# Down projection of the ConvFFN by seven block products, with block sums made by accumulating transfers

## The chip, the cores and the metric

The kernel runs on one core of a Trainium2 chip. The metric is the device time of one execution in microseconds. Before the change the median of three runs is 1632.61 us (1627.53 to 1633.84).

## The reference, cut to what matters

One layer over 1024 latent tokens of width 1024: modulated input, two attention branches (a windowed and a global one), gates, output projection, LayerNorm, then a gated ConvFFN with D_FF = 2816 and a second LayerNorm. The change lies in the ConvFFN.

```python
def _conv_ffn(h, w_up, conv_w, conv_b, w_down):
    u = h @ w_up                                   # (1024, 5632)
    u = conv_of_width_3_over_tokens(u) + conv_b
    gate, val = jnp.split(u, 2, axis=-1)
    return (jax.nn.silu(gate) * val) @ w_down      # (1024, 2816) @ (2816, 1024)

h = x * (1.0 + scale2) + shift2
y = _conv_ffn(h, w_up[l], conv_w[l], conv_b[l], w_down[l])
x = _layer_norm(DEEPNORM_ALPHA * x + gate2 * y, ln2_g[l], ln2_b[l])
```

## The kernel before, in words

Everything is kept transposed, with features on the 128 partitions and tokens along the row. A product of fp32 matrices is made of three matmuls (`mm3`, L85 to L88): each operand is split into a rounded high part, cast on ACT (L78), and the low rest, a subtraction on DVE or POOL (L83), and high by high, high by low and low by high are summed in one PSUM bank.

The program goes through projections, 32 attention units (`Unit`, L378; 16 of the windowed branch, then 16 of the global one, in a loop over u that interleaves the steps of scores, values and filling work), branch merge, LN1, and the ConvFFN. In an attention unit SP writes a row of sums to DRAM (`dn`, L497), reads it back spread over partitions (`rb`, L499) and fetches rotated queries (L402, L403); POOL scales outputs (`ot`, L559), splits queries (`qs`) and makes one of the probability tiles (`pth`, `ptl`), which PE multiplies next.

The up projection makes 22 tiles of 128 gate and 128 value features. Tiles 0 to 2 are made directly (`up_conv`). Tiles 3 to 21 (`up_tile`, L1292) are made by seven products of blocks instead of eight, named A11, S2, S3, S1, A12, S4 and A22, 12 matmuls of 512 columns each: weights come by SP (`ru`, L1257), POOL forms the sums of weight blocks (`wsums`, L1041) and the low parts of S4 and A22 (`wS`, `wA`, L83), DVE forms the other low parts and adds the products to each other (L1288), ACT copies banks out (`pe`), POOL adds the last pair (`uv`), ACT and DVE do the convolution (`conv3`, L1176 to L1179) and SiLU, and `gated` (L1182) multiplies gate by value on DVE and stores the tile of 128 features by 1024 tokens in DRAM (`gd`, L1184). Work tiles in SBUF (`ht`, given back by `hput`) are slots reused in turn, six per up tile.

The down projection, y = gated @ w_down, runs in two parts. First half of the tokens: a loop over the 22 k-tiles (`acc`, shown as `ya`) adds into eight PSUM banks, 528 matmuls of 512 columns; each k-tile's weights (512 KB, `rwd`) and both token halves of `gd` (`rg`) are loaded by SP and split; the second half is kept split in SBUF (`gr`). Second half (`rest`, shown as `yl`): output tiles f = 0 to 3 by 264 matmuls of 512 columns, then f = 4 to 7 in two slices of 256 tokens by 528 matmuls of 256 columns, with all weights loaded a second time in another layout (`w_dnf`, `rwf`). `accum` (ACT and DVE) adds the residual `zz`; LN2 of finished parts runs beside the matmuls (`ln_steps`, let forth by `tick`, with distances LN2_D and LN2_E); the last 256 tokens are transposed by PE (`tok`), measured by DVE and written out.

The order of PE's instructions is that of the code (L1137: a manual schedule for PE); the other engines' instructions are placed by a scheduler, and waits follow from the buffers.

## Time and profile before

| what | us |
|---|---|
| median of three runs | 1632.61 |
| the profiled execution | 1630.69 |
| its span in the profile | 1628.9 |
| PE busy in the span | 1563.2 |
| up projection by block products, tiles 3 to 21 | about 1002 to 1363 |
| down projection, first half of the tokens | 1363.6 to 1483.2 |
| down projection, second half | 1483.2 to 1613.7 |
| end after the last product | 1613.7 to 1628.9 |

The profiled execution took 1.8 us more than its span, at a granted TensorE clock of 0.991, and lies 1.9 us under the median. In rows of the trace the first two numbers are the start and the length of a group of equal instructions; what stands in brackets at the end is the idle time of that engine just ahead and what ended it.

### The profile page before, as it was taken

What the parts mean: (1) busy time and instruction counts of PE and PEld (TensorE: products, weight loads), DVE (VectorE), ACT (ScalarE), POOL (GpSimd) and SP (SyncE); (2) the same over time, 40 slices, a digit from 0 to 9 for tenths busy, and PEclk for the clock granted to TensorE, in tenths of its full rate; (3) what the DMA queues carried; (4) which work ended last, traced back from release to release, by engine and by line L of the source; (5) the groups of instructions that cost most, each with busy time, mean ns of one, the idle gap of its engine ahead of it and who ended that gap; (6) DMA issues with size and microseconds to landing.
All of it is one profiled execution on the core that took longest, in us unless ns stands there. A gap on an engine that the chain in (4) does not pass through costs nothing.

```text
span 1628.9 us, 22394 instructions
## 1 busy us (share of the span) xinstructions
PE 1563.2 (96%) x7944; PEld 1303.5 (80%) x7944; DVE 1173.0 (72%) x1692; ACT 813.5 (50%) x1468; POOL 844.0 (52%) x756
## 2 busy tenths in 40 slices
PE   6999999999999999999999989999999999999996
PEld 5878788888877887777788877888888888888896
DVE  7797646548887677887756695899999996335445
ACT  5322222358887667777223563444444444443343
POOL 0573302526665555655225353666776663337785
PEclk9999999999999999999999999999999999999998
DMA  9695662322230111011440211222222228653453
GB/s 379 211 318 179 213 206 84 117 74 60 61 100 21 46 33 46 24 27 61 158 155 32 99 65 65 78 78 78 78 80 89 88 97 301 218 189 96 149 164 110
DMA packets 86801, 192.52 MB, mean 118 GB/s; under 512 B 11040, under 2 KB 25888, under 8 KB 86688
## 3 DMA queue, kind: packets, MB, share of 16 engines
q1 hardware_dynamic: 81648, 181.63, 33.7%
q10 hardware_dynamic: 5040, 9.46, 1.6%
q8 instruction: 62, 1.02, 0.2%
q14 instruction: 51, 0.42, 0.1%
HBM read 154.28 MB, written 28.38 MB: 112 GB/s over the span
## 4 chain that ended last, share of the span: by engine, by line
PE 80%; DVE 7%; ACT 4%; DMA 3%; issue 3%; POOL 2%; SPq 0%; ACTq 0%; DVEq 0%; POOLq 0%
PE ptr L524 5%; PE g L86 3%; PE g L87 3%; PE g L88 3%; PE b L88 3%; PE b L87 3%; PE b L86 3%; PE ya L88 2%; PE ya L87 2%; PE ya L86 2%; PE av L545 2%; PE av L546 2%; PE d L86 2%; PE d L87 2%; PE yl L86 2%
## 5 line engine op out<-in xcount | busy, mean ns | idle before, releaser
L534 DVE TENSOR_TENSOR ptl<-ptr,pth 128x512 fp32r<-128x512 f32 x188 | 125.0, 685 | 22.5 <-ACT pth L533 19.8
L533 ACT CAST pth<-ptr 128x512 fp32r<-128x512 f32 x188 | 106.7, 587 | 63.7 <-PE ptr L524 37.6
L524 PE MATMUL ptr<-ident,p 128*128 128x128 f32 x816 | 127.2, 278 | 7.0 <-DVE ptl L534 5.1
L420 ACT ACTIVATE p<-p,nm 128x1024 f32<-128x1024 f32 (+2 forms) x128 | 125.3, 981 | 5.6 <-DVE p L453 4.6
L524 PEld LDWEIGHTS ptr<-ident,p 128*128 128x128 f32 x816 | 94.0, 140 | 36.7 <-DVE ptl L534 13.1
L545 PE MATMUL av<-pth,VT 128*128 128x512 f32 x236 | 104.4, 442 | 0.7 <-ACT avs L551 0.5
L83 POOL TENSOR_TENSOR wlg<-wg,whg 128x512 fp32r<-128x512 f32 x32 | 44.8, 1407 | 112.9 <-ACT whg L78 112.9
L86 PE MATMUL g<-hh,whg 128*128 128x512 f32 x256 | 99.9, 390 | 0.0
L88 PE MATMUL g<-hh,wlg 128*128 128x512 f32 x256 | 99.7, 390 | 0.0
L87 PE MATMUL g<-hl,whg 128*128 128x512 f32 x256 | 99.6, 389 | 0.0
L546 PE MATMUL av<-ptl,VT 128*128 128x512 f32 x236 | 97.6, 414 | 2.0 <-POOL ptl L83 1.8
L453 DVE TENSOR_SCALAR_CACHE_REDUCE p<-s,cvt,nmc 128x1024 f32<-128x1024 f32 x64 | 84.3, 1339 | 13.4 <-PE s L409 13.2
L83 POOL TENSOR_TENSOR lwf<-rwf,hwf 128x1024 fp32r<-128x1024 f32 (+1 forms) x36 | 82.3, 2302 | 12.4 <-ACT hwf L78 12.4
L86 PE MATMUL yl<-gr,hwf 128*128 128x256 f32 (+1 forms) x264 | 85.4, 323 | 0.0
L88 PE MATMUL yl<-gr,lwf 128*128 128x256 f32 (+1 forms) x264 | 84.2, 319 | 0.1
L87 PE MATMUL yl<-gr,hwf 128*128 128x256 f32 (+1 forms) x264 | 84.0, 318 | 0.0
L408 PE MATMUL s<-KL,q 128*128 128x512 f32 (+2 forms) x192 | 76.1, 396 | 5.1 <-ACT p_x L420 4.3
L83 POOL TENSOR_TENSOR lwd<-rwd,hwd 128x1024 fp32r<-128x1024 f32 x16 | 38.8, 2423 | 75.0 <-ACT hwd L78 60.6
L80 POOL TENSOR_SCALAR pth<-prw 128x512 fp32r<-128x512 f32 x48 | 30.1, 628 | 90.3 <-ACT prw L530 64.8
L182 DVE CUSTOM_DVE_ANT_0 wml<-wml,sc,bmc 128x1024 f32<-128x1024 f32 x32 | 44.6, 1406 | 40.1 <-DMA wml<-in_wmodT_dram 39.8
L409 PE MATMUL s<-KL,q 128*128 128x512 f32 (+2 forms) x192 | 71.5, 373 | 0.0
L1288 POOL TENSOR_TENSOR uv<-ve,pe 128x512 f32<-128x512 f32 x19 | 29.9, 1573 | 77.2 <-DVE ve L1288 38.1
(387 smaller groups left out, 5295.3 us busy)
## 6 DMA issues: line engine op xcount, KB each, us to landing
wml<-in_wmodT_dram SPq DMA_DIRECT2D x48, 512.0 KB
ru<-in_w_up_dram SPq DMA_DIRECT2D x38, 512.0 KB
rwf<-in_w_dnf_dram SPq DMA_DIRECT2D x24, 512.0 KB
rg<-gd SPq DMA_DIRECT2D x44, 256.0 KB
rwd<-in_w_dn_dram SPq DMA_DIRECT2D x22, 512.0 KB
gd<-tg SPq DMA_DIRECT2D x19, 512.0 KB
wm<-in_wmodT_dram SPq DMA_DIRECT2D x16, 512.0 KB
wg<-in_w_g_dram SPq DMA_DIRECT2D x32, 256.0 KB
```

The source lines that it names most:

```text
L83: lo_eng.tensor_tensor(out=lo, in0=src, in1=hi.bitcast(F32), op=ALU.subtract)
L86: nc.tensor.matmul(ps, a[0], b[0], start=start, stop=False, skip_group_check=resumed)
L87: nc.tensor.matmul(ps, a[0], b[1], start=False, stop=False, skip_group_check=resumed)
L88: nc.tensor.matmul(ps, a[1], b[0], start=False, stop=stop, skip_group_check=resumed)
L408: nc.tensor.matmul(o, self.q[0][:, hs], ks, start=True, stop=False)
L420: nc.scalar.activation(p, s, AF.Exp, bias=nm[:, h:h + 1], scale=scale, accum_out=sm[:, h:h + 1])
L453: nc.vector.tensor_scalar(out=p, in0=o, scalar1=self.qscale(nqs)[:, hs] if self.br else -1.0, scalar2=self.other[:, hs], op0=ALU.mult, op1 ...
L524: nc.tensor.transpose(tr[:, h * P:(h + 1) * P], self.pslice(h, n), ident)
L533: nc.scalar.copy(hi, tr)
L534: nc.vector.tensor_tensor(out=lo, in0=tr, in1=hi.bitcast(F32), op=ALU.subtract)
L545: nc.tensor.matmul(self.av, v, hi, start=first, stop=False)
L546: nc.tensor.matmul(self.av, v, lo, start=False, stop=self.left == 0)
```

## The change

The down projection becomes seven block products with the input dimension outermost. The 22 k-tiles are cut in two halves of 11 (tile k and tile k+11), the outputs in f = 0 to 3 and 4 to 7, the tokens in two halves; product p multiplies one weight block or sum of blocks by one block, or sum, of the gated activations, over 11 k-steps and four output tiles (12 matmuls of 512 columns per k-step). Products 1, 6, 2, 7, 4 and 5 run so, in this order, on two alternating sets of four banks; product 3 comes last, in two slices of 256 tokens. `accum` and `accum_affine` add each product to the outputs it belongs to, with the gain's sign turned where needed (`nmod`); intermediates `u2` and `u3` stay in SBUF. The second copy of the weights, `w_dnf`, is gone. On PE the list has 7422 rows where it had 7686: 264 matmuls of 256 columns less.

The sums are made by transfers. **Weights:** `wd_sums` is called at nine units of the attention loop (DNS: u = 3, 6, 9, 11, 14, 17, 19, 22, 25); each call has SP copy weight blocks (1 MB, or 0.75 MB) to a new DRAM tile `sd`, and POOL issue an accumulating transfer onto it: 12 in all. **Gated blocks:** `gated` stores tiles 0 to 10 by two SP transfers (three copies of the first token half, one of the second), and POOL accumulates the second half onto two of them; tiles 11 to 21 are negated by the product on DVE, stored once (`g2d`), and accumulated by POOL onto tile j-11: 22 in all. In product 4 the second operand gets one more accumulating transfer per k-step, from `g2d` into SBUF: 11. Before the change POOL issued no transfer.

In the up tile S1 comes ahead of S3, one slot `pv` takes the place of `pe` and `ve` (five slots per tile instead of six), ACT copies c into `uv`, DVE adds d to it, and POOL adds the rest. Each k-step of a product loads 256 KB of weights and 256 KB of gated blocks into one raw tile (`dload`), three steps ahead (DAH); seven of product 3's eleven pairs are loaded early (D3AT). In the listings below each row has a line of the code, the operation, output and inputs.

**POOL in a steady up tile.** `s` are sums of weight blocks, `wA` and `wS` low parts of A22 and S4, `uv` the value half; td_82 belongs to tile 3, uv_10657 to tile 4. Before:

```order
L83 TENSOR_TENSOR wS_4_10660<-s_4_10529,wS_4_10660 128x512
L1041 TENSOR_TENSOR s_5_10670<-ru_5_10667 128x512
L1041 TENSOR_TENSOR s_5_10671<-ru_5_10666,ru_5_10667 128x512
L1041 TENSOR_TENSOR s_5_10670<-s_5_10670,ru_5_10666 128x512
L83 TENSOR_TENSOR wA_4_10663<-ru_4_10525,wA_4_10663 128x512
L1041 TENSOR_TENSOR s_5_10671<-ru_5_10666,s_5_10670 128x512
L1288 TENSOR_TENSOR uv_10615<-ve_10613,pe_10612 128x512
L83 TENSOR_TENSOR wS_5_10802<-s_5_10671,wS_5_10802 128x512
```

and now:

```order
L87 TENSOR_TENSOR wS_4_10702<-s_4_10570,wS_4_10702 128x512
L1075 TENSOR_TENSOR s_5_10712<-ru_5_10709 128x512
L1075 TENSOR_TENSOR s_5_10713<-ru_5_10708,ru_5_10709 128x512
L1075 TENSOR_TENSOR s_5_10712<-s_5_10712,ru_5_10708 128x512
L87 TENSOR_TENSOR wA_4_10705<-ru_4_10566,wA_4_10705 128x512
L1075 TENSOR_TENSOR s_5_10713<-ru_5_10708,s_5_10712 128x512
L1246 DMA td_82<-tg_10515 128x2x512
L1354 TENSOR_TENSOR uv_10657<-uv_10657,pv_10655 128x512
L87 TENSOR_TENSOR wS_5_10845<-s_5_10713,wS_5_10845 128x512
```

A transfer onto `td` of tile 3 now stands between the last weight sum and the `uv` of tile 4, and waits for that tile's two stores.

**POOL in the attention**, units of the windowed branch. `qs` are split queries, `pth` and `ptl` a probability tile, `ot` and `O` outputs. Before:

```order
L559 TENSOR_TENSOR ot_0_0_3299<-ot_0_0_3299,rb_0_0_3131 128x256
L80 TENSOR_SCALAR O_3303<-ot_0_0_3299 128x2x128
L83 TENSOR_TENSOR O_3304<-ot_0_0_3299,O_3303 128x2x128
L80 TENSOR_SCALAR qs_3_0_3538<-Q_2_1032 128x4x64
L83 TENSOR_TENSOR qs_3_0_3538<-Q_2_1032,qs_3_0_3538 128x4x64
L80 TENSOR_SCALAR pth_1_0_3_3410<-prw_1_0_3_3412 128x512
L553 TENSOR_SCALAR up_0_1_3420<-avs_0_1_3418 64x512
L83 TENSOR_TENSOR ptl_1_0_3_3411<-prw_1_0_3_3412,pth_1_0_3_3410 128x512
```

and now, at the same place, u = 3:

```order
L566 TENSOR_TENSOR ot_0_0_3299<-ot_0_0_3299,rb_0_0_3131 128x256
L601 DMA sd_0_3447<-in_w_dn_dram 512x1x512
L84 TENSOR_SCALAR O_3303<-ot_0_0_3299 128x2x128
L84 TENSOR_SCALAR qs_3_0_3544<-Q_2_1032 128x4x64
L87 TENSOR_TENSOR O_3304<-ot_0_0_3299,O_3303 128x2x128
L87 TENSOR_TENSOR qs_3_0_3544<-Q_2_1032,qs_3_0_3544 128x4x64
L84 TENSOR_SCALAR pth_1_0_3_3410<-prw_1_0_3_3412 128x512
L560 TENSOR_SCALAR up_0_1_3420<-avs_0_1_3418 64x512
L87 TENSOR_TENSOR ptl_1_0_3_3411<-prw_1_0_3_3412,pth_1_0_3_3410 128x512
```

The transfer onto `sd` stands behind `ot`, ahead of the split of the output `O`, of the next unit's `qs` and of the next `ptl`. On SP the copy that it waits for stands between `dn` and `rb` of such a unit.

**DVE in the down projection.** `ld` are low parts of a loaded pair, `lwd`, `g` and `gr` their counterparts before, `zz` the residual. Before, in the first half:

```order
L83 TENSOR_TENSOR lwd_13604<-rwd_13601,hwd_13603 128x1024
L83 TENSOR_TENSOR gr_13676<-rg_1_13677,gr_13676 128x512
L83 TENSOR_TENSOR g_13607<-rg_0_13608,g_13607 128x512
L83 TENSOR_TENSOR gr_13716<-rg_1_13717,gr_13716 128x512
L83 TENSOR_TENSOR g_13647<-rg_0_13648,g_13647 128x512
L83 TENSOR_TENSOR gr_13756<-rg_1_13757,gr_13756 128x512
L83 TENSOR_TENSOR g_13687<-rg_0_13688,g_13687 128x512
L83 TENSOR_TENSOR gr_13796<-rg_1_13797,gr_13796 128x512
```

and now, from the end of product 2 to the first additions of its results:

```order
L87 TENSOR_TENSOR ld_9_13847<-rd_9_13843,hd_9_13846 128x1024
L87 TENSOR_TENSOR ld_10_13866<-rd_10_13862,hd_10_13865 128x1024
L87 TENSOR_TENSOR ld_0_13892<-rd_0_13888,hd_0_13891 128x1024
L87 TENSOR_TENSOR ld_3_14008<-rd_3_14004,hd_3_14007 128x1024
L87 TENSOR_TENSOR ld_1_13911<-rd_1_13907,hd_1_13910 128x1024
L1412 SCALAR_TENSOR_TENSOR zz_0_13215<-p_0_13692,nmod,zz_0_13215 128x512
L1412 SCALAR_TENSOR_TENSOR zz_0_13217<-p_1_13693,nmod,zz_0_13217 128x512
L1412 SCALAR_TENSOR_TENSOR zz_0_13219<-p_2_13694,nmod,zz_0_13219 128x512
L1418 SCALAR_TENSOR_TENSOR zz_1_13216<-zz_1_13216,lnx,ya_13929 128x512
L996 TENSOR_TENSOR zq_13228<-zq_13228,sqb_0_13933 128x512
L1412 SCALAR_TENSOR_TENSOR zz_0_13221<-p_3_13695,nmod,zz_0_13221 128x512
L87 TENSOR_TENSOR ld_2_13963<-rd_2_13959,hd_2_13962 128x1024
```

One low part of 1024 columns per k-step takes the place of one or two smaller ones and of POOL's; the additions from four banks stand together with the sums of LN2 and splits between them.

The diff, cut to its core:

```diff
-LN2_E = 4500.0, 4500.0, 2500.0, 1500.0, 700.0
+LN2_E = 3500.0, 3000.0, 1500.0, 800.0, 500.0
+DAH = 3
+D3AT = (2, 2), (2, 5), (2, 8), (7, 2), (7, 5), (7, 8), (5, 0)
+NXS = 5
+DNS = {u0 + 3 * n: (n, j0, j1) for u0, j0, j1 in ((3, 0, 4), (11, 4, 8), (19, 8, 11)) for n in range(3)}
...
+    def wd_sums(n, j0, j1):
+        def a(r, c):
+            return w_dn[c * NH + j0:c * NH + j1][:, :, 4 * r:4 * r + 4].rearrange("n p f q -> p n (f q)")
+
+        def put(key, src, *more):
+            tag = tokens.pop()
+            t = dpool.tile([P, j1 - j0, HALF], F32, tag=tag, name=f"sd{key}_{j0}")
+            for j in range(j0, j1):
+                sd[key, j] = t[:, j - j0]
+            sd[key] = t
+            nc.sync.dma_start(t, src)
+            for m in more:
+                nc.gpsimd.dma_start(t, m, accum_op=ALU.add)
+
+        if n == 0:
+            put(1, a(1, 0), a(1, 1))
+            put(3, a(0, 0), a(1, 0))
+        elif n == 1:
+            put(2, sd[1], a(0, 0))
+        else:
+            put(4, sd[2], a(0, 1))
 
...
+        if u in DNS:
+            wd_sums(*DNS[u])
...
+    def dsrc(p, k):
+        w = w_dn[k], w_dn[NH + k]
+        lo, hi = slice(0, 4), slice(4, 8)
+        return {1: (w[0][:, lo], td[k][:, 0]), 6: (sd.get((2, k)), td[k][:, 2]),
+                2: (w[1][:, lo], g2d[k][:, 0:HALF]), 7: (sd.get((3, k)), td[k][:, 3]),
+                4: (w[1][:, hi], td[k][:, 2]), 5: (sd.get((1, k)), td[k][:, 1]),
+                3: (sd.get((4, k)), g2d[k][:, HALF:T])}[p]
+
+    def dload(p, k, mk):
+        w, g = dsrc(p, k)
+        n = nraw[0] % (3 + len(xs))
+        nraw[0] += 1
+        pool, tag, bufs = (post, "raw", 3) if n < 3 else (*xs[n - 3], 1)
+        r = pool.tile([P, 2, HALF], F32, tag=tag, name=f"rd{p}_{k}", bufs=bufs)
+        o = r[:, 0]
+        nc.sync.dma_start(o.rearrange("p (a b) -> p a b", b=P) if len(w.shape) == 3 else o, w)
+        nc.sync.dma_start(r[:, 1], g)
+        if p == 4:
+            nc.gpsimd.dma_start(r[:, 1], g2d[k][:, 0:HALF], accum_op=ALU.add)
+        h, l = (mk(f"{a}d{p}_{k}", (P, 2, HALF), R32) for a in "hl")
+        split(r, h, l, nc.scalar, nc.vector)
+        return h, l
+
+    nraw = [0]
+    xs = []
+    dseq = [(p, k) for p in (1, 6, 2, 7, 4, 5) for k in range(NH)]
+    dq = []
+
+    def dnext():
+        if len(dq) < DAH and dseq:
+            dq.append(dload(*dseq.pop(0), ring))
...
     def gated(j, tg, tv):
-        nc.vector.tensor_tensor(out=tg, in0=tg, in1=tv, op=ALU.mult)
-        nc.sync.dma_start(gd[j], tg)
+        lo, hi = tg[:, 0:HALF], tg[:, HALF:T]
+        if j < NH:
+            nc.vector.tensor_tensor(out=tg, in0=tg, in1=tv, op=ALU.mult)
+            nc.sync.dma_start(td[j][:, 0:3], twice(lo, 3))
+            nc.sync.dma_start(td[j][:, 3], hi)
+            nc.gpsimd.dma_start(td[j][:, 1:3], twice(hi), accum_op=ALU.add)
+        else:
+            nc.vector.scalar_tensor_tensor(out=tg, in0=tg, scalar=-1.0, in1=tv, op0=ALU.mult, op1=ALU.mult)
+            nc.sync.dma_start(g2d[j - NH], tg)
+            nc.gpsimd.dma_start(td[j - NH][:, 2:4], twice(hi), accum_op=ALU.add)
 
...
     def up_tile(j):
         a, b, c, d = (bank(f"{n}{j}") for n in "abcd")
-        pe, ve = ht(f"pe{j}", (P, 2, HALF)), ht(f"ve{j}", (P, 2, HALF))
+        pv = ht(f"pv{j}", (P, 2, HALF))
+        pe, ve = pv[:, 0], pv[:, 1]
         ug, uv, tg, tv = (ht(f"{n}{j}") for n in ("ug", "uv", "tg", "tv"))
         prod(j, "A11", a, True, True)
-        nc.scalar.copy(pe[:, 0], a)
+        nc.scalar.copy(pe, a)
         prod(j, "S2", b, True, True)
-        add(ve[:, 0], b, pe[:, 0])
-        prod(j, "S3", d, True, True)
-        add(ve[:, 1], d, ve[:, 0])
+        add(ve, b, pe)
+        prod(j, "S1", c, True, True)
+        nc.scalar.copy(uv[:, hihalf], c)
         pairs(j, "A12", "S4", "A22")
         if j + 1 < NF:
             wload(j + 1)
             wsums(j + 1, tm)
-        prod(j, "S1", c, True, True)
-        nc.scalar.copy(pe[:, 1], c)
-        add(uv[:, hihalf], ve[:, 1], pe[:, 1], nc.gpsimd)
+        prod(j, "S3", d, True, True)
+        add(uv[:, hihalf], d, uv[:, hihalf])
+        add(uv[:, hihalf], uv[:, hihalf], ve, nc.gpsimd)
         pairs(j + 1, "A11")
         prod(j, "A12", a, False, True)
         nc.scalar.copy(ug[:, lohalf], a)
         prod(j, "S4", c, False, True)
-        add(ug[:, hihalf], c, ve[:, 0])
+        add(ug[:, hihalf], c, ve)
         conv3(tg, ug, j)
         nc.scalar.activation(tg, tg, AF.Silu)
-        pairs(j + 1, "S2", "S3", "S1")
+        pairs(j + 1, "S2", "S1", "S3")
         prod(j, "A22", d, False, True)
-        add(uv[:, lohalf], d, ve[:, 0])
+        add(uv[:, lohalf], d, ve)
         conv3(tv, uv, NF + j)
         gated(j, tg, tv)
-        hput(*[f"{n}{j}" for n in ("pe", "ug", "ve", "uv", "tg", "tv")])
+        hput(*[f"{n}{j}" for n in ("pv", "ug", "uv", "tg", "tv")])
 
...
+    def product(p):
+        tags = sides[nside[0] % 2]
+        nside[0] += 1
+        acc = [ps4.tile([P, HALF], F32, tag=f"r{n}", name=f"p{p}_{f}") for f, n in enumerate(tags)]
+        for k in range(NH):
+            dnext()
+            dnext()
+            if (p, k) in D3AT:
+                d3.append(dload(3, len(d3), ht))
+            h, l = dq.pop(0)
+            for f in range(4):
+                c = slice(f * P, (f + 1) * P)
+                mm3(acc[f], (h[:, 0, c], l[:, 0, c]), (h[:, 1], l[:, 1]), k == 0, k == NH - 1)
+                tick(HALF / 0.8)
+        return acc
+
...
+    for p in (1, 6, 2, 7, 4, 5):
+        if p == 6:
+            for hf in (0, 1):
+                for k in range(4):
+                    for a in (0, 1):
+                        nc.sync.dma_start(zt_[k, hf][:, a], zd[k + 4 * a][:, hsl(hf)])
             for a in (0, 1):
                 nc.sync.dma_start(lnr[a], ln2_row[a].partition_broadcast(P))
+        if p == 5:
+            banks[:] = sides[nside[0] % 2 ^ 1]
+        acc = product(p)
+        for f in range(4):
+            o = acc[f]
+            if p == 1:
+                nc.scalar.copy(u2[f], o)
+            elif p == 6:
+                accum(f, h0, u2[f], False)
+                nc.vector.tensor_tensor(out=u2[f], in0=u2[f], in1=o, op=ALU.subtract)
+            elif p == 2:
+                accum(f, h0, o, True)
+                sums(f, h0, f == 0)
+                accum_affine(f, h1, u2[f], True)
+            elif p == 7:
+                nc.vector.tensor_tensor(out=u3[f], in0=u2[f], in1=o, op=ALU.add)
+                accum(f + 4, h0, u3[f], True)
+                accum_affine(f + 4, h1, u3[f], False)
+            elif p == 4:
+                accum(f + 4, h0, o, True)
+                sums(f + 4, h0, False)
+            else:
+                accum(f + 4, h1, o, False)
+                sums(f + 4, LN2_S[1], f == 0)
+        if p == 7:
+            hput("u20", "u21", "u30", "u31")
+        if p == 4:
+            pend += ln_steps(zs2, zq2, h0, "b0", emit2, *LN2_D, LN2_P[0])
+    for f in range(4):
+        accum(f, h1, acc[f], True)
+    banks[:] = sides[nside[0] % 2] + sides[nside[0] % 2 ^ 1]
+    d3 += [dload(3, k, ring) for k in range(len(D3AT), NH)]
 
...
+    todo = [4, 5, 6, 7]
+    for r in LN2_S[1:]:
+        q = slice(r.start - HALF, r.stop - HALF)
+        for f in range(4):
+            o = sml(f"yl{f}_{r.start}")[:, 0:r.stop - r.start]
+            c = slice(f * P, (f + 1) * P)
+            for k, (h, l) in enumerate(d3):
+                mm3(o, (h[:, 0, c], l[:, 0, c]), (h[:, 1, q], l[:, 1, q]), k == 0, k == NH - 1)
+                tick((r.stop - r.start) / 0.8)
+            accum(f, r, o, True)
+            if r.stop < T:
+                sums(f, r, False)
+                if f == 3:
+                    pend += ln_steps(zs2, zq2, r, "b1", emit2, *LN2_E, LN2_P[1])
+            if todo:
+                tok(todo.pop(0))
+            if r.stop == T:
+                todo.append(f)
+    hput(*[f"{a}d3_{k}" for k in range(len(D3AT)) for a in "hl"])
+    hfree += xs
+    tok(3)
```

More of the change, by code (lines that the diff above doesn't have):

```diff
@@ new lines, in layer_kernel @@
+    nmod = post.tile([P, 8], F32, tag="nmod", name="nmod")
+    nc.vector.tensor_scalar(out=nmod, in0=modc[:, 40:48], scalar1=-1.0, scalar2=None, op0=ALU.mult)
+    hfree[:] = hfree[7:] + hfree[:7]
+    xs += [hfree.pop(0) for _ in range(NXS)]
+    lnr = ht("lnr", (P, 2, HALF)), ht("lnr2", (P, 2, HALF))
+    for k in range(4):
+        for hf in (0, 1):
+            zt_[k, hf] = ht(f"zz{k}_{hf}", (P, 2, HALF))
+    u2 = [ht(f"u2{n}", (P, 2, HALF)) for n in (0, 1)]
+    u2 = [u2[f // 2][:, f % 2] for f in range(4)]
@@ L1557, in _arrange @@
         w_dn=A(dn),
-        w_dnf=A(tiles(w_dn)),
         rope_c=A(cs.reshape(NT, P, HD).transpose(1, 0, 2)),
```

126 lines of the change are left out of this document (37 added, 89 removed).

## The prediction, made before the changed kernel ran

> **What bounds the kernel now.** I read the page's busy times first, then windows by stage (PE, PEld, DVE, ACT and POOL busy with counts, clock, DMA share, GB/s), then the rows of single stages.
>
> ```profile
> PE 1563.2 (96%) x7944; PEld 1303.5 (80%) x7944; DVE 1173.0 (72%) x1692; ACT 813.5 (50%) x1468; POOL 844.0 (52%) x756
> 1100.00:1200.00 100.00, 100.00 (x443) 82.80 (x442) 92.68 (x72) 48.38 (x69) 69.79 (x38) 1.00 0.23 79
> 1363.00:1425.00 62.00, 62.00 (x276) 51.32 (x275) 28.78 (x32) 26.87 (x36) 19.57 (x8) 1.00 0.75 259
> 1425.00:1483.00 58.00, 58.00 (x257) 48.04 (x256) 22.02 (x26) 23.81 (x33) 23.15 (x11) 1.00 0.50 162
> 1483.00:1548.00 65.00, 65.00 (x297) 53.35 (x296) 34.75 (x29) 25.29 (x34) 55.62 (x32) 1.00 0.41 132
> 1548.00:1614.00 66.00, 65.91 (x545) 65.33 (x544) 33.37 (x33) 30.41 (x45) 55.33 (x31) 1.00 0.50 150
> ```
>
> PE is busy without a gap through the up projection and the whole down projection, at clock 1.00. There the end is set by the count and pitch of matmuls, and anything taken from PE is taken from the end as long as no other engine comes late. In the down projection DVE is busy 22 to 29 us in some 60, so it has room; in the up projection it is 93% busy and POOL 70%, so those two have little. DMA reaches 259 GB/s at a share of 0.75.
>
> **What the change removes.** The pitch of a matmul is read from starts, since lengths overlap:
>
> ```profile
> L86 PE MATMUL ya<-g,hwd x176: 389/389/389, 1363.6 to 1482.6; 128*128 128x512 f32 x176
> L88 PE MATMUL ya<-g,lwd x176: 389/389/389, 1364.0 to 1483.0; 128*128 128x512 f32 x176
> ...
> 1548.29 0.28 PE L87 MATMUL yl<-gr,hwf 128*128 128x256 f32 x1
> ...
> 1549.97 0.28 PE L86 MATMUL yl<-gr,hwf 128*128 128x256 f32 x1
> ```
>
> The 528 matmuls of 512 columns start from 1363.6 to 1483.0: (1483.0 − 1363.6) / 527 = 0.2266 us. The 256-wide ones start 14 pitches apart from 1548.29 to 1549.97: 0.120 us. Before there are 792 wide and 528 narrow; after, six products of 11 × 12 = 132 wide make 792, and product 3 makes 11 × 12 × 2 = 264 narrow. So 264 narrow ones go, 264 × 0.120 = **31.7 us**; small matmuls of LN2 and the transposes stay. This is the only gain on PE. The time of the second weight copy's loads and splits was hidden beside a full PE and gives nothing.
>
> **What it adds in the down projection.** A k-step is 12 × 0.2266 = 2.72 us of PE. It needs one cast and one subtraction of 128x1024:
>
> ```profile
> L78 ACT CAST hwd<-rwd 128x1024 fp32r<-128x1024 f32 x19 | 19.9, 1047 | 0.0
> L83 DVE TENSOR_TENSOR lwd<-rwd,hwd 128x1024 fp32r<-128x1024 f32 x5 | 6.1, 1226 | 1.3 <-ACT hwd L78 1.3
> L1352 DVE SCALAR_TENSOR_TENSOR zz<-ya,modc,zz 128x512 f32<-128x512 f32 x5 | 3.5, 748 | 5.0 <-PE ya L88 5.0
> L962 DVE TENSOR_TENSOR zq<-zq,sqb 128x512 f32<-128x512 f32 x1 | 1.1, 1105 | 0.0
> ```
>
> ACT 1.05 and DVE 1.23 of 2.72 us fit. Around the evacuation of product 2 DVE has 8 additions of 0.75 us, 4 `zq` of 1.1 and, with three early pairs of product 3, some 14 subtractions of 1.23 in product 7's 30 us: 6 + 4.4 + 17.2 = 28 us. That is nearly full, with three pairs (8.2 us of PE) ready ahead; I take nothing, up to 10 us. A load is 512 KB per k-step: 0.524 MB / 2.72 us = 193 GB/s, under the 259 that the trace shows; product 4's further 256 KB read and written back adds a half and more on 11 steps only. Nothing is taken for DMA either.
>
> The start of product 1 has to get by tile 21's leftovers on DVE:
>
> ```profile
> 1217.04 2.31 DVE L1177 SCALAR_TENSOR_TENSOR tv<-uv,cvt,tv 128x1023 f32<-128x1023 f32 x1
> 1219.39 2.20 DVE L1179 SCALAR_TENSOR_TENSOR tv<-uv,cvt,tv 128x1023 f32<-128x1023 f32 x1
> 1223.21 1.21 DVE L1183 TENSOR_TENSOR tg<-tg,tv 128x1024 f32<-128x1024 f32 x1
> ...
> 1230.50 1.28 DVE L1177 SCALAR_TENSOR_TENSOR tg<-ug,cvt,tg 128x1023 f32<-128x1023 f32 x1 [1.37 <-ACT tg L1176]
> ```
>
> Two steps of 1.28, then 2.31, 2.20 and 1.21: 8.3 us of DVE, against 8.2 us of PE in the pairs ready. So 0 to 8; I take **2**, because the scheduler sets the leftovers between the splits.
>
> **What it adds in the up projection.** The steady tile lasts 19.04 us:
>
> ```profile
> 1210.46:1229.50 19.04, 19.04 (x86) 15.77 (x85) 17.89 (x14) 8.78 (x14) 12.85 (x7) 1.00 0.22 80
> ...
> 1213.03 1.30 POOL L1041 TENSOR_TENSOR s<-ru 128x512 f32<-128x512 f32 x1 [2.65 <-DMA ru<-in_w_up_dram]
> ...
> 1220.46 2.28 POOL L1041 TENSOR_TENSOR s<-ru,s 128x512 f32<-128x512 f32 x1
> 1226.37 1.61 POOL L1288 TENSOR_TENSOR uv<-ve,pe 128x512 f32<-128x512 f32 x1 [3.63 <-DVE ve L1288]
> 1232.33 2.40 POOL L1041 TENSOR_TENSOR s<-ru 128x512 f32<-128x512 f32 x1 [2.65 <-DMA ru<-in_w_up_dram]
> ...
> 1224.45 0.33 SPq L1184 DMA_DIRECT2D gd<-tg  x1
> 1228.59 0.33 SPq L1257 DMA_DIRECT2D ru<-in_w_up_dram  x1
> ...
> 1234.64 0.57 ACT L1297 COPY pe<-a 128x512 f32<-128x512 f32 x1
> ```
>
> POOL has 19.04 − 12.85 = 6.2 us to spare. The accumulating transfer of the tile just gated stands between POOL's sum that ends at 1222.7 and `uv` at 1226.37. For tiles up to 10 it first waits for SP's stores, issued from 1224.45. The nearest landing is `ru`: 512 KB issued at 1228.59, used at 1232.33, at most 3.74 us; the 768 KB store by proportion 5.6. So POOL is let go at 1228.5 to 1230.4, then `uv` 1.6 us, when ACT's next convolution step wants it by about 1232.5. That just holds.
>
> Behind it stands the reuse of the slot. With five slots per tile, the one of tile j's `tg` becomes `pv` two tiles later in the order of the program, which in time is the copy at 1234.64, 10 us after the multiplication. The accumulating transfer must have read its source by then. A copy that waits holds ACT, and the bank that A12 accumulates into: PE stops when the copy starts later than about 1239.8 (A12 follows 48 matmuls, 10.9 us, into the tile that starts at 1229.50; the copy takes 0.57). From the let-go at 1230.4, with about 1 us of issue, that leaves some **8.4 us** for an accumulating transfer in tiles 3 to 10; tiles 11 to 21 wait only for DVE, done at 1224.4, and have 6.0 more, 14.4. The trace has no such transfer. From below, 3.74 us as one load of that size: no wait. From above, it reads its source, reads its target and writes it, three times 3.74 = 11.2: 8 × 2.8 = 22 us. I take **2**, nearest to the single load, since the three parts can overlap. Its issue on POOL, never seen either, is bounded by SP's 0.33 from below and POOL's longest row, 2.4, from above.
>
> The Trainium skill speaks to this in "DMA: Bandwidth & Descriptors", section "Anatomy of one DMA — SWDGE (gpsimd) path": about 2.0 us plus bytes / 436 GB/s for a transfer issued by GpSimd; an estimate by it is 3.2 us for 512 KB, which would make this term zero. No row of before shows one.
>
> **What it adds in the attention.** A windowed unit takes about 8.36 us:
>
> ```profile
> 398.87 0.62 POOL L80 TENSOR_SCALAR pth<-prw 128x512 fp32r<-128x512 f32 x1 [1.05 <-ACT prw L530]
> 399.45 0.74 POOL L559 TENSOR_TENSOR ot<-ot,rb 128x256 f32<-128x256 f32 x1
> 400.15 1.29 POOL L83 TENSOR_TENSOR ptl<-prw,pth 128x512 fp32r<-128x512 f32 x1
> ...
> 404.24 0.41 POOL L80 TENSOR_SCALAR qs<-Q 128x256 fp32r<-128x256 f32 x1 [1.61 <-PE qtr L398]
> ...
> 407.23 0.62 POOL L80 TENSOR_SCALAR pth<-prw 128x512 fp32r<-128x512 f32 x1 [1.06 <-ACT prw L530]
> ...
> PE av L546 <- POOL ptl L83: 1.8, 2, 1.4
> ```
>
> POOL is idle about 1.05 + 1.6 us of a unit, and PE has waited for `ptl` only twice in the whole attention (the waits of PE between 358 and 780), 1.8 us together. Twelve accumulating transfers are put into POOL's queue here, ahead of `O`, `qs` and the next `ptl`. An issue of 0.33 us is hidden by the gap ahead of `pth`; one of 2.4 would pass it by about 1.4, and 12 × 1.4 = 17. I take **3**, a quarter of a microsecond each, since the issue rows of SP lie near the lower end. SP's copy between `dn` and `rb` holds SP some 0.3 to 1 us; `rb` is needed only by `ot`.
>
> The end loses one ACT step of 0.56 us behind the last product but has LN2 of the tokens before closer to it: taken as −1, −1 to +2.
>
> **Sum.** 1630.69 − 31.7 + 2 + 2 + 3 − 1 = 1605.0; rounded up for waits of under a microsecond, **1606**. That is against the profiled execution, 1.9 us under the median, so about 1608 beside the median; I keep 1606, since the three runs lie 6 us apart.
>
> **Rivals.** *POOL as the new hold* (the issue is 1 to 2.4 us, `ptl` and `uv` come late): start 4, attention 10, up 6 give 1619, somewhere between 1613 and 1632. For it: POOL in attention has gaps of 1 to 1.6 us only. Against: it idles 3.6 us ahead of `uv` in each up tile.
>
> *Transfers land late* (the slower side; one place, the `pv` copy on ACT and A12 on PE behind it). Each up tile from 3 to 10 then lasts (L − 8.4) us longer and from 11 on (L − 14.4), L being the time from issue to landing. It eats the gain from L = 8.4 + 31.7 / 8 = 12.4 us; at L = 16 it costs 8 × 7.6 + 11 × 1.6 = 78 us: 1630.7 − 31.7 + 78 = 1677. For it: DVE is 93% busy, and POOL's rows of one shape vary from 1.3 to 2.3 us beside it, so what POOL does is held up by DVE; if making the transfer's list on POOL is held up likewise, L grows. Against: the one landing of this size that rows bound is under 3.74 us.
>
> The Trainium skill has that rule in "SBUF — State Buffer", section "Who interferes with whom" and the box on the "DVE blocks DMA" trap: a GpSimd-issued transfer starves while DVE runs in a two-port mode. The same section says that `tensor_tensor` has no such mode and with two inputs only meets GpSimd's reads, and the DVE rows of the up tile quoted here have two inputs. The differing lengths of POOL's rows agree with the second part; the first would show as the late landing just priced.
>
> *The down projection becomes bound by loads or DVE* (both token-half blocks come from DRAM now, 77 loads): if rates stay at 162 instead of 193 GB/s, k-steps last 3.24 us, 66 × 0.52 = 34 us, and the gain is gone: 1605 + 34 = 1639.
>
> *It does not do what it says*: the counted list of PE rows is short by exactly 264, so this is out.
>
> **How the numbers follow.** Forecast 0.57 (1598 to 1613), POOL as hold 0.19, late transfers 0.14, loads or DVE 0.10 (1620 to 1645). 0.5% of 1632.6 is 8.2 us, about what a measurement of this kernel can tell from no change. Faster, below 1624.4: 0.57 + three quarters of 0.19 + a fifth of 0.10, 0.73. Slower, above 1640.8: 0.14 + a quarter of 0.10, 0.16. Between: 0.11. The range, 1597 to 1640, takes in −31.7 with all terms at nothing and a little over the unknown costs of attention and up tile together (17 + 22 − 31.7 = +7); what it leaves out is the late transfers and the tail of the loads.
>
> **What would show it.** PE in the down projection: without a gap and 31.7 us shorter, from the end of A22 of tile 21 to the last product some 218 us instead of 250. Up tiles of 19.04 us in the steady stretch, both in tiles 3 to 10 and after; a wait of PE on `pv` in 4 to 12 would speak for late transfers. Attention units of 8.36 us also at u = 3, 6, 9, 11; waits of `av` on `ptl` there for POOL. Wrong would be a landing of over 8.4 us, gaps on PE waiting for `ld`, or a down stage whose pitch is not 0.2266 us.

## The result, and the profile after

The changed kernel takes 1642.51 us (median of 8 runs, 1637.69 to 1648.34) against 1632.31 us of the kernel before beside it: ratio 1.0068, 95% interval 1.0047 to 1.0088. It is slower by about 10 us, where 26 us less were forecast. The profiled execution took 1638.73 us, 3.8 under that median; its span of 1637.0 us is 8.1 more than before, and the account below is of these 8.1 us.

The page's busy times:

```profile
PE 1542.5 (94%) x7680; PEld 1277.7 (78%) x7680; DVE 1208.5 (74%) x1748; ACT 810.8 (50%) x1443; POOL 728.0 (44%) x749
```

Windows of the up projection (two) and of the down projection (four), columns as in the prediction:

```profile
1100.00:1200.00 100.00, 92.56 (x386) 74.44 (x386) 89.11 (x64) 39.24 (x58) 46.65 (x38) 0.96 0.49 127
1250.00:1350.00 100.00, 100.00 (x443) 82.84 (x442) 81.38 (x74) 47.60 (x69) 69.39 (x42) 1.00 0.46 114
1387.00:1508.00 121.00, 120.97 (x534) 99.86 (x533) 78.63 (x73) 59.38 (x63) 10.43 (x9) 1.00 0.81 265
1508.00:1538.00 30.00, 25.88 (x106) 20.63 (x105) 19.56 (x23) 13.46 (x16) 6.03 (x7) 0.94 0.92 247
1538.00:1577.00 39.00, 39.00 (x178) 31.85 (x177) 30.15 (x33) 17.55 (x21) 11.18 (x8) 1.00 0.42 136
1577.00:1622.00 45.00, 38.23 (x293) 37.20 (x292) 26.61 (x50) 15.02 (x27) 18.98 (x19) 0.92 0.18 63
```

PE has 264 instructions less and is no longer full: 7.4 us of 100 are missing in the first up window, none in the second; in the down projection 4.1 us in one window and 6.8 us in the last. In the windows with a gap the clock is under 1.00 too. What PE waited for from 1000 us on (total, times, longest):

```profile
PE a L90 <- ACT pv L1364: 12.2, 7, 2.5
PE p L91 <- DVE ld L87: 4.1, 2, 3.9
PE yl L90 <- ACT hd L82: 3.4, 1, 3.4
PE yl L91 <- DVE ld L87: 3.3, 1, 3.3
```

Reading the same marks (starts of matmuls at the borders of the stages, to 0.1 us, so that a difference can be off by 0.1) in both traces gives the account, in us:

| stage | before | after | difference |
|---|---|---|---|
| up to the first score matmul | 344.9 | 342.5 | −2.4 |
| attention, first to last score | 409.7 | 417.1 | **+7.4** |
| merge, output projection, LN1 | 162.6 | 162.3 | −0.3 |
| direct up tiles 0 to 2 | 77.3 | 79.0 | +1.7 |
| tile 3 | 25.6 | 24.2 | −1.4 |
| up tiles 4 to 12 | 171.4 | 191.2 | **+19.8** |
| up tiles 13 to 21 | 172.2 | 171.4 | −0.8 |
| down projection | 249.9 | 233.9 | **−16.0** |
| end | 15.4 | 15.4 | 0 |

The sum is +8.0 of the 8.1 us. Nine up tiles are read from the start of A11 of tile 4 to that of tile 13:

```profile
1020.06 0.39 PE L86 MATMUL a<-B,wA 128*128 128x512 f32 x1
...
1191.42 0.39 PE L86 MATMUL a<-B,wA 128*128 128x512 f32 x1
```

before, and after:

```profile
1025.13 0.39 PE L90 MATMUL a<-B,wA 128*128 128x512 f32 x1
...
1216.34 0.39 PE L90 MATMUL a<-B,wA 128*128 128x512 f32 x1
```

In these tiles, one period of the changed kernel on POOL, DVE, SP, ACT and PE reads so (from A12 of tile 6 into tile 7; the lines are ordered by engine):

```profile
1069.42 1.72 POOL L1075 TENSOR_TENSOR s<-ru,s 128x512 f32<-128x512 f32 x1
1083.04 1.20 POOL L1246 DMA_DIRECT2D td<-tg  x1 [11.90 <-DMA td<-tg]
1083.82 1.75 POOL L1354 TENSOR_TENSOR uv<-uv,pv 128x512 f32<-128x512 f32 x1
1085.07 1.75 POOL L87 TENSOR_TENSOR wS<-s,wS 128x512 fp32r<-128x512 f32 x1
...
1091.30 1.73 POOL L1075 TENSOR_TENSOR s<-ru,s 128x512 f32<-128x512 f32 x1
...
1062.76 9.48 DVE L1232 SCALAR_TENSOR_TENSOR tg<-ug,cvt,tg 128x1023 f32<-128x1023 f32 x1 [1.38 <-ACT tg L1231]
1077.66 1.22 DVE L1243 TENSOR_TENSOR tg<-tg,tv 128x1024 f32<-128x1024 f32 x1
1083.86 10.27 DVE L1232 SCALAR_TENSOR_TENSOR tg<-ug,cvt,tg 128x1023 f32<-128x1023 f32 x1 [1.37 <-ACT tg L1231]
...
1078.91 0.38 SPq L1244 DMA_DIRECT2D td<-tg  x1
1079.34 0.48 SPq L1245 DMA_DIRECT2D td<-tg  x1
...
1072.93 1.24 ACT L1231 ACTIVATE tv<-uv,cvt 128x1024 f32<-128x1024 f32 x1 [8.90 <-DVE uv L1354]
1075.09 0.57 ACT L1364 COPY pv<-a 128x512 f32<-128x512 f32 x1
...
1075.70 0.50 PE L90 MATMUL a<-B,wA 128*128 128x512 f32 x1 [1.46 <-ACT pv L1364]
```

POOL stands 11.9 us at its accumulating transfer, until the stores issued at 1078.91 and 1079.34 have landed at 1083.04: for the first 7.7 us the product of the gated tile is not done on DVE (its row starts at 1077.66 and lasts 1.22 us), and the last 4.2 us are the stores. Then it has seven operations to do and does them with no gap, one every 1.24 us, to 1093.0. At 1083.86, just behind POOL's first, DVE comes to a convolution step that takes 1.28 us elsewhere; its row lasts 10.27 us and ends at 1094.1, one such step behind POOL's last. The step before, at 1062.76, shows what follows from it: ACT waits 8.9 us for the next addition on DVE, the `pv` copy stands behind that on ACT, and PE waits for `pv`. Seven such waits, in tiles 6 to 12, make 12.2 us; behind the three of 2.4 to 2.5 us the matmuls also start 0.43 us apart for some 3.4 us, as behind the long wait shown under x6_nop4, and not behind those of 0.9 to 1.7. The theory (**W**): POOL's wait for the stores piles its queue up, and the piled-up run keeps DVE's operations with two inputs in SBUF out. The rivals: the transfers land late (**L**, the prediction's), or the issue of a transfer on POOL itself holds DVE up (**G**).

### The profile page after: what moved, and what is told of

It is laid out like the page before. It is cut to its first block, busy times and chain, and to the rows that moved or that the text cites. A ratio compares the mean times of both kernels' runs of the same rounds, so it can differ in the third digit from the quotient of the medians.

```text
span 1637.0 us, 22064 instructions
## 1 busy us (share of the span) xinstructions
PE 1542.5 (94%) x7680; PEld 1277.7 (78%) x7680; DVE 1208.5 (74%) x1748; ACT 810.8 (50%) x1443; POOL 728.0 (44%) x749
## 3 DMA queue, kind: packets, MB, share of 16 engines
q0 software_dynamic: 13392, 25.96, 10.3%
## 4 chain that ended last, share of the span: by engine, by line
PE 66%; DVE 16%; ACT 5%; issue 5%; DMA 4%; POOL 3%; ACTq 0%; SPq 0%; DVEq 0%; POOLq 0%
DVE tg L1232 4%; PE ptr L531 4%; PE p L91 3%; PE p L90 3%; PE p L92 3%; PE g L92 3%; PE g L90 3%; PE g L91 3%; PE b L91 2%; PE b L92 2%; PE b L90 2%; PE av L553 2%; PE av L552 2%; PE s L414 2%; PE a L90 2%
## 5 line engine op out<-in xcount | busy, mean ns | idle before, releaser
L87 DVE TENSOR_TENSOR ld<-rd,hd 128x1024 fp32r<-128x1024 f32 x77 | 93.3, 1234 | 56.8 <-ACT hd L82 53.1
L82 ACT CAST hd<-rd 128x1024 fp32r<-128x1024 f32 x77 | 80.0, 1050 | 97.1 <-PE p L92 52.4
L1232 DVE SCALAR_TENSOR_TENSOR tg<-ug,cvt,tg 128x1023 f32<-128x1023 f32 x19 | 88.9, 4677 | 25.9 <-ACT tg L1231 25.9
L91 PE MATMUL p<-ld,hd 128*128 128x512 f32 x264 | 103.6, 392 | 4.2 <-DVE ld L87 4.1
L90 PE MATMUL p<-hd 128*128 128x512 f32 x264 | 104.0, 394 | 0.0
L92 PE MATMUL p<-hd,ld 128*128 128x512 f32 x264 | 103.4, 392 | 0.0
L90 PE MATMUL a<-B,wA 128*128 128x512 f32 x152 | 62.0, 408 | 12.2 <-ACT pv L1364 12.2
```

The source lines that it names most:

```text
L87: lo_eng.tensor_tensor(out=lo, in0=src, in1=hi.bitcast(F32), op=ALU.subtract)
L90: nc.tensor.matmul(ps, a[0], b[0], start=start, stop=False, skip_group_check=resumed)
L91: nc.tensor.matmul(ps, a[0], b[1], start=False, stop=False, skip_group_check=resumed)
L92: nc.tensor.matmul(ps, a[1], b[0], start=False, stop=stop, skip_group_check=resumed)
L1232: nc.vector.scalar_tensor_tensor(out=t[:, 1:T], in0=u[:, 0:T - 1], scalar=cvw[:, c, 0:1], in1=t[:, 1:T], op0=ALU.mult, op1=ALU.add)
```

## The experiments

Those up to x8 each start from the changed kernel; x9_early9 goes on from x5_global, and x10_all and x11_spread each from x9_early9. Stages are read by the marks of the table.

### x1_noacc: without the accumulating transfers of tiles 0 to 10

```diff
             nc.sync.dma_start(td[j][:, 3], hi)
-            nc.gpsimd.dma_start(td[j][:, 1:3], twice(hi), accum_op=ALU.add)
```

> Leaves out the accumulating transfers of gated tiles 0 to 10 (their stores stay), so products 6, 5 and part of the others read sums that lack the second token half. In the changed kernel the nine tiles 4 to 12 of the up projection take 191.2 us where 9 x 19.04 = 171.4 would do. Theory W (POOL waits at this transfer for the two stores, some 12 us per tile, its queue piles up, and the piled-up operations then run back to back and shut DVE's two-input operations out): the nine tiles take 171 to 173 us, no DVE row of tg is longer than 2.4 us, span about 1617. Rival L (the transfers land late and the slot of pv is not free): the same 171. Rival D (what costs is the extra stored and loaded data or the five slots per tile, not the accumulation): 185 or more.

Nine up tiles: 171.4 us, every one 19.04; span 1620.8, one run at 1622.76 us. The longest `tg` step on DVE is 2.2 us. So the accumulation costs the 19.8 us and not the stored data or the five slots.

### x2_aside: the same transfers without the wait

```diff
+    side8 = dpool.tile([P, 8, P], F32, tag="side", name="side")
+    nc.sync.dma_start(side8, w_dn[0])
+    side = side8.rearrange("p (a b) q -> p a (b q)", a=2)
...
-            nc.gpsimd.dma_start(td[j][:, 1:3], twice(hi), accum_op=ALU.add)
+            nc.gpsimd.dma_start(side, twice(hi), accum_op=ALU.add)
```

> The accumulating transfers of gated tiles 0 to 10 keep their size, source and place in POOL's queue, but add onto a spare block in DRAM that nobody stores to, so they wait for DVE's product only and not for the two stores; the sums in td are left out. Theory W (the wait in POOL's queue is the cost): nine up tiles in 171 to 174 us, DVE's tg rows at 1.3 to 2.4 us, span about 1617 to 1619. Rival L (landing of the transfer and reuse of its slot) and rival G (making the transfer on POOL keeps DVE out of SBUF by itself): 185 to 192 us as in the changed kernel, with the long tg rows.

Nine up tiles: 171.4 us; span 1618.9, one run at 1620.66 us. The convolution step on DVE (count, shortest, median and longest ns), first of the changed kernel, then of x2_aside:

```profile
L1232 DVE SCALAR_TENSOR_TENSOR tg<-ug,cvt,tg x19: 1282/1304/10455, 1024.7 to 1387.5; 128x1023 f32<-128x1023 f32 x19
```

```profile
L1232 DVE SCALAR_TENSOR_TENSOR tg<-ug,cvt,tg x19: 1282/1283/1285, 1027.5 to 1370.4; 128x1023 f32<-128x1023 f32 x19
```

And the issues of the accumulating transfers in the list of DMAs (count, size, median us to landing), the changed kernel's and then x2_aside's:

```profile
td<-tg POOLq DMA_DIRECT2D x19, 512.0 KB, 6.6
```

```profile
side<-tg POOLq DMA_DIRECT2D x8, 512.0 KB, 8.2
```

POOL's wait at this place is now 1.4 to 4.4 us, 1.4 in five of the eight tiles, for DVE's product alone. Rival G is out, since POOL issues as many transfers at the same place. Against L speaks that they took longer from issue to landing here (8.2 us) at no cost; but they were issued sooner behind the product, so the changed kernel's own rows decide: there ACT never waits for a transfer ahead of a `pv` copy. (In x2_aside it did once, for 0.6 us, where a landing took 9.7 us.) What is left is the wait in POOL's queue. That the piled-up run is what holds DVE is read from the rows, and no run takes the pile away and leaves the wait. The rows of all eight tiles agree, though: the long step on DVE ends 2.8 us behind the start of the last POOL operation of the run, whether DVE came to it early in the run (10.3 us long, above) or with the third of the seven operations under way, as here, behind the transfer of tile 3:

```profile
1043.71 6.77 DVE L1232 SCALAR_TENSOR_TENSOR tg<-ug,cvt,tg 128x1023 f32<-128x1023 f32 x1 [1.37 <-ACT tg L1231]
...
1047.69 1.71 POOL L1075 TENSOR_TENSOR s<-ru,s 128x512 f32<-128x512 f32 x1
```

### x3_poolsum: POOL adds in SBUF, SP stores the sum

```diff
-            nc.sync.dma_start(td[j][:, 0:3], twice(lo, 3))
+            nc.sync.dma_start(td[j][:, 0], lo)
             nc.sync.dma_start(td[j][:, 3], hi)
-            nc.gpsimd.dma_start(td[j][:, 1:3], twice(hi), accum_op=ALU.add)
+            add(tv[:, 0:HALF], lo, hi, nc.gpsimd)
+            nc.sync.dma_start(td[j][:, 1:3], twice(tv[:, 0:HALF]))
```

> Same result by another way: for gated tiles 0 to 10 POOL adds the two token halves in SBUF and SP stores the sum twice; no accumulating transfer and no wait for a store in POOL's queue. Theory W: POOL waits for DVE's product only, nine up tiles in 171 to 174 us, span about 1617, 1619 us in time, ratio to the kernel before about 0.992. Rival P (POOL has no room for one more operation of 1.3 to 2.4 us beside DVE): up tiles of 20 us or more, nine in 180 or more.

1627.47 us (10 runs) against 1634.06, ratio 0.9964 (0.9948 to 0.9981), span 1624.0. The nine tiles take 171.4 us, so POOL has the room; but tile 3 took 28.9 us instead of 24.0, which ate 5 us of it and is most of what the expected span of about 1617 was missed by. PE waits there 6.8 us (2.3 in the changed kernel) for a cast on ACT, and the cast, by the profile, for the stores of the last direct tile, one of which SP now issues only behind POOL's addition:

```profile
1014.33 1.04 ACT L1113 CAST T24h<-t 128x1024 fp32r<-128x1024 f32 x1 [6.60 <-DMA td<-c]
```

### x4_noasum: the weight sums without their accumulation

```diff
             nc.sync.dma_start(t, src)
-            for m in more:
-                nc.gpsimd.dma_start(t, m, accum_op=ALU.add)
```

> Leaves out the twelve accumulating transfers of weight blocks in the attention (SP's copies stay), so the weight sums hold their first block only. In the changed kernel the attention, from the first to the last score matmul, takes 416.8 us against 409.5 before. Theory W (POOL held at these transfers by the copies' landing): 409 to 411 us, span about 1630. Rival S (SP's copies of 1 MB stand ahead of the small reads of dn and rb in the same queue and make these late): 414 to 417, little changed.

Attention 409.5 us, as before the change; span 1630.9, one run at 1632.71 us. SP's copies alone cost nothing, rival S is out. In the changed kernel the loss is mostly at one place: followed score by score, 4.8 of the 7.4 us arise between 443 and 450 us, behind this wait (POOL and SP):

```profile
439.03 1.17 POOL L601 DMA_DIRECT2D sd<-in_w_dn_dram  x1 [4.55 <-DMA sd<-in_w_dn_dram]
...
427.31 0.61 SPq L599 DMA_DIRECT2D sd<-in_w_dn_dram  x1
```

The copy of 1 MB issued at 427.31 had landed only 11.7 us later.

### x5_global: both repaired, the weight sums moved to longer units

```diff
-DNS = {u0 + 3 * n: (n, j0, j1) for u0, j0, j1 in ((3, 0, 4), (11, 4, 8), (19, 8, 11)) for n in range(3)}
+DNS = {u0 + n: (n, j0, j1) for u0, j0, j1 in ((17, 0, 4), (20, 4, 8), (23, 8, 11)) for n in range(3)}
...
-            nc.sync.dma_start(td[j][:, 0:3], twice(lo, 3))
...
-            nc.gpsimd.dma_start(td[j][:, 1:3], twice(hi), accum_op=ALU.add)
+            if j < NCL:
+                nc.sync.dma_start(td[j][:, 0:3], twice(lo, 3))
+                nc.gpsimd.dma_start(td[j][:, 1:3], twice(hi), accum_op=ALU.add)
+            else:
+                nc.sync.dma_start(td[j][:, 0], lo)
+                add(tv[:, 0:HALF], lo, hi, nc.gpsimd)
+                nc.sync.dma_start(td[j][:, 1:3], twice(tv[:, 0:HALF]))
```

> Two edits: gated sums of tiles 3 to 10 by POOL in SBUF (tiles 0 to 2 as in the changed kernel), and the weight sums moved from units 3 to 25 of the attention to units 17 to 25, which are nearly all of the global branch and longer. Theory W (the attention loses where a copy of 1 MB has not landed when POOL comes to the transfer onto it, in the short windowed units): attention 411 to 414 us instead of 417.1, nine up tiles 171.4, span about 1615 to 1619. Rival H (each of the twelve transfers costs by its 1.15 us hold of POOL, wherever it stands): attention stays at 416 to 418.

1615.43 us (4 runs) against 1632.30, ratio 0.9896 (0.9871 to 0.9920), span 1615.4. Attention 411.6, nine tiles 171.4, tile 3 24.1. Rival H is out as a price per transfer; whether the longer units hide the hold of 1.15 us or only the landing was not told apart. The down projection is as in the changed kernel: 189.6 us for the six products ahead of product 3, that is 1, 6, 2, 7, 4 and 5 ("products 1 to 5" from here on), and 44.0 for the two slices of product 3.

### x6_nop4: product 4 without its accumulation

```diff
-        if p == 4:
-            nc.gpsimd.dma_start(r[:, 1], g2d[k][:, 0:HALF], accum_op=ALU.add)
```

> Leaves out the eleven accumulating transfers of product 4 into SBUF, so its second operand lacks one block. Theory C (the chain load, accumulation of 7.4 us, cast, subtraction is too long for what is read ahead): PE's wait of 3.9 us for ld in product 4 and the slower matmuls behind it go, products 1 to 5 take 183 to 185 us instead of 189.8. Rival E (the additions of product 7's results stand ahead of the subtractions in DVE's queue): a wait of 3 us or more remains, 188 or more.

Products 1 to 5: 183.5 us instead of 189.8, PE's wait in product 4 gone, the waits at product 3's start unchanged; one run at 1633.34 us. Theory C holds and rival E falls. In the changed kernel these transfers of 256 KB take 7.4 us to land:

```profile
rd<-g2d POOLq DMA_DIRECT2D x11, 256.0 KB, 7.4
```

The wait costs more than its length. PE's rows behind it, in the changed kernel:

```profile
1520.68 0.50 PE L91 MATMUL p<-ld,hd 128*128 128x512 f32 x1 [3.88 <-DVE ld L87]
...
1521.38 0.63 PE L90 MATMUL p<-hd 128*128 128x512 f32 x1
1521.81 0.63 PE L91 MATMUL p<-ld,hd 128*128 128x512 f32 x1
1522.23 0.63 PE L92 MATMUL p<-hd,ld 128*128 128x512 f32 x1
...
1524.37 0.45 PE L91 MATMUL p<-ld,hd 128*128 128x512 f32 x1
1524.65 0.40 PE L92 MATMUL p<-hd,ld 128*128 128x512 f32 x1
```

For 3.7 us the matmuls start 0.43 us apart instead of 0.2266: about 1.7 us more. The granted clock of that window is 0.94. The Trainium skill, "TensorE: Matmul & The Clock Gate", Part 1, says that PE's clock falls to half after an idle window of about 3.4 us and comes back after as long a busy one, with starts 426.7 ns apart at 512 columns when cold; the trace agrees with 0.43 us. In the length of the wait it differs: the waits of 2.4 to 2.5 us on `pv` were enough here, those of up to 1.7 us were not.

### x7_ln2late and x8_ln2early: LN2's output steps moved

```diff
-LN2_D = 16000.0, 5000.0, 2500.0, 1500.0, 700.0
+LN2_D = 26000.0, 5000.0, 2500.0, 1500.0, 700.0
```

and 7000.0 in x8_ln2early.

> One number: LN2 of the first token half is let forth 26 us instead of 16 us behind product 4, so its eight output steps on ACT stand behind the casts of product 3's last pairs. Theory Q (these casts come late because they are queued behind the output steps): the two waits at product 3's start, 3.4 and 3.3 us, shrink to 2 us together, the two slices take 36 to 39 us instead of 44.1, span about 1630. Rival R (the last pairs' slots come free only when product 5 ends, whatever the queue): the slices stay at 43 or more.

> The same number the other way: 7 us instead of 16, so the output steps are done beside product 5. Theory Q: slices at 36 to 39 us as with the late one, unless product 5 now waits for its own pairs (then products 1 to 5 above 191). Rival R: 43 or more.

Late: 1646.10 us (4 runs) against 1632.30, ratio 1.0084 (1.0052 to 1.0115), slices 48.9. Early: one run at 1646.62, slices 39.2, but products 1 to 5 201.5. The wait for `hd` at product 3's start did go in the late one, but the one for `ld` became 3.8 us, and one of 3.6 us came, of LN2's `stb` for POOL: theory Q's number fell. The early one's proviso came true instead: product 5 waits for its own pairs (3.8 us for `hd`). So the queue of ACT is one of several things around product 5's end, and moving one moves the wait.

### x9_early9: nine pairs of product 3 early, on top of x5_global

```diff
-D3AT = (2, 2), (2, 5), (2, 8), (7, 2), (7, 5), (7, 8), (5, 0)
+D3AT = (2, 2), (2, 5), (2, 8), (7, 2), (7, 5), (7, 8), (5, 0), (5, 3), (5, 6)
```

> On top of x5_global one edit: nine instead of seven of product 3's pairs are loaded and split early, in slots that u2 and u3 have given back, so that only the last two have to go through the ring that product 5 still uses. Theory B (the late pairs are held by product 5's end together with the operations queued behind that end: eight additions on DVE, the output steps of LN2 on ACT): the two waits of 3.4 and 3.3 us at product 3's start go, the slices take 35 to 37 us instead of 44.0, span about 1607. Rival V (DVE and ACT are simply too loaded around product 5's end, as the runs with an earlier and a later LN2 suggest): a wait of 3 us or more turns up elsewhere, products 1 to 5 above 191 or slices above 40, span 1612 or more.

Slices 34.6 us instead of 44.0, both waits there gone; products 1 to 5 194.3 instead of 189.6, with waits for `ld` of 3.9 us in product 4 and 3.1 in product 5. Span 1606.8, one run at 1608.58 us. Theory B holds for the slices, and a part comes back as V said.

### x10_all: product 4's block added by POOL in SBUF

```diff
...
         if p == 4:
-            nc.gpsimd.dma_start(r[:, 1], g2d[k][:, 0:HALF], accum_op=ALU.add)
+            if k % 2 == 0:
+                r2[0] = raw(f"rg{k}")
+                for a in range(min(2, NH - k)):
+                    nc.sync.dma_start(r2[0][:, a], g2d[k + a][:, 0:HALF])
+            add(r[:, 1], r[:, 1], r2[0][:, k % 2], nc.gpsimd)
...
+        if p == 5:
+            d3 += [dload(3, k, ring) for k in range(len(D3AT), NH)]
...
-    d3 += [dload(3, k, ring) for k in range(len(D3AT), NH)]
```

> On top of x9_early9: in product 4 the extra block is loaded by SP into a slot of its own and added by POOL in SBUF, instead of the accumulating transfer (the loads of product 3's last two pairs also come ahead of product 5's additions in the program). Theory C: the chain is shorter by some 5 us, PE's wait in product 4 goes, products 1 to 5 take 183 to 185 us instead of 189.6, span about 1600, ratio to the kernel before 0.979 to 0.984. Rival: the extra slots and loads make the pairs late again, products 1 to 5 at 188 or more.

1611.82 us (6 runs) against 1628.84, ratio 0.9893 (0.9875 to 0.9911). The profiled execution is the slowest of the six, at 1618.84. In it products 1 to 5 take 199.1 us, and 192 would be left if all of the 7.0 us over the median lay there: the expectation fell, the rival's number held. Product 4 itself went from 37.2 us in x9_early9 to 33.9, but product 5 from 36.8 to 44.9, and the longest wait for `ld` is there:

```profile
1537.64 0.80 PE L91 MATMUL p<-ld,hd 128*128 128x512 f32 x1 [6.27 <-DVE ld L87]
```

The extra loads take half a slot more per pair of the eight raw slots, and the loads of product 3's last two pairs now stand ahead of product 5's additions. Which of the two delays product 5 was not told apart; that slots are the limit is tested by the next run.

### x11_spread: the early pairs out of product 7, on top of x9_early9

```diff
-D3AT = (2, 2), (2, 5), (2, 8), (7, 2), (7, 5), (7, 8), (5, 0), (5, 3), (5, 6)
+D3AT = (6, 2), (6, 5), (6, 8), (2, 2), (2, 5), (2, 8), (2, 10), (5, 4), (5, 8)
```

> On top of x9_early9 one table: the early pairs of product 3 are loaded in products 6 and 2 (seven) and 5 (two), none in product 7, so that product 4's pairs are read ahead while product 7 runs. Theory C (product 4's chain of load, accumulation, cast and subtraction is late because the slots ahead of it are taken): the waits on ld in products 4 and 5, 7.7 us in x9_early9, fall to 3 us or less, products 1 to 5 take 184 to 189 us instead of 194.3, slices stay at 34 to 35, span 1597 to 1603, ratio 0.978 to 0.983. Rival A (the chain's length, with the accumulation's 7.4 us in it, is what is too long, whatever goes ahead): waits of 5 us or more, products 1 to 5 above 190.

1604.61 us (5 runs, 1599.04 to 1608.06) against 1635.52, **ratio 0.9807 (0.9783 to 0.9831)**. Products 1 to 5 take 185.0 us with the accumulating transfers in place (product 4 now 29.9), slices 34.6: theory C's numbers came, rival A's did not. The accumulations still land after 7.2 us here. The page's busy times, and then PE's waits from 1360 us on:

```profile
PE 1535.9 (96%) x7680; PEld 1274.9 (80%) x7680; DVE 1187.5 (74%) x1748; ACT 813.0 (51%) x1443; POOL 763.5 (48%) x749
```

```profile
PE p L91 <- DVE ld L87: 0.9, 2, 0.5
PE zt L1531 <- DVE zz L1417: 0.4, 1, 0.4
```

The down projection is 219.6 us, 30.3 less than before; PE's waits in it are down to 0.9 us ahead of the end.

## Why the prediction was wrong

**The gain on PE, 31.7 us: right.** 264 narrow matmuls are gone, and with the waits removed the down projection is 30.3 us shorter (x11_spread). In the changed kernel 16.0 of it were left.

**The up projection, 2 us taken: the step that failed.** The prediction saw POOL held until 1228.5 to 1230.4 and concluded of the `uv` behind it "That just holds". It asked only when the next operand of that one operation is wanted, and then priced another thing, the reuse of the slot (landing over 8.4 us). Landing was 6.6 us, under that, and in x2_aside 8.2 with next to no harm. What it left out is what stands behind the waiting instruction as a whole: seven operations of POOL, which then run without a gap, and DVE, whose convolution step does not end until they are through. The rows for it were quoted (POOL's operations of one shape at 1.30 and 2.28 us beside DVE) and read only as a price of POOL's. 19.8 us were lost: 12.2 us of waits on `pv`, and the rest in slow starts behind them, 4.9 of it where these are 0.43 us apart. A wait of PE on `pv` in tiles 4 to 12 had been named as a sign of late transfers. It was seen, in 6 to 12, and did not mean that.

**The attention, 3 us taken, 0 to 17 given: mis-sized, 7.4.** The issue held POOL 1.15 us, inside the bounds. The 4.8 us at one place come from a copy that landed after 11.7 us; the prediction wrote of SP's copy only how long it holds SP, not when it lands.

**The down projection, nothing taken for loads and DVE: wrong, 15.7 us.** Some 6.3 us are product 4 (x6_nop4), where a load is followed by an accumulation of 7.4 us before the cast can start; the prediction counted bytes per microsecond and not the length of the chain against the pairs that can be ahead; with other pairs out of its way the same chain cost nothing (x11_spread). The other 9.4 are product 3's start (44.0 to 34.6 in x9_early9): four of its pairs go through slots that product 5 still uses, and with two of these four loaded early both waits were gone. The prediction did not look at the slots of the last product.

**The start of product 1, 2 us: nothing lost there**; PE has no wait between 1387 and 1513 in the changed kernel. **The end, −1: 0.**

**The rivals.** None came as described. The slower outcome was put at 0.16, and at 1677 us for a landing that was not late; it came by three losses of 7 to 20 us, where the sum had 2, 3 and nothing. The nearest was POOL as the new hold: the issue of 1.15 to 1.2 us lies in its bounds and its 10 us for the attention are not far from 7.4, but its 6 us for the up tiles stood for a late `uv` and not for DVE held up. x11_spread, with the three repaired, runs 30.9 us under the kernel before beside it (1635.52 to 1604.61), more than the 26 forecast, and so close to the 31.7 counted on PE. That 1604.61 lies beside the forecast's 1606 is in part luck: the kernel before took 3.2 us more in that series than in the one of the result (1632.31).

## What to carry to other kernels

A transfer that waits for another one does not belong in the queue of an engine that has computing to do: list what stands behind it, what those operations will do when they come at once, and whom they hold up. An accumulating transfer takes the place of an addition only where its landing, 6 to 10 us here, fits the look-ahead; one operation more on POOL was cheaper than one transfer with a wait. A wait of PE of 2.4 us or more cost 1.5 us or more on top here.
